# When the samples' steps over the cached values are issued during the prompt's attention

## The chip, the cores and the metric

The kernel runs on one core of one Trainium2 chip. The metric is the time of one whole execution in microseconds (us) as the device measures it; the median of several executions is quoted. The engines are named as the profile names them: PE (TensorE: matrix products), DVE (VectorE), ACT (ScalarE), POOL (GpSimd) and SP (SyncE, which here only starts transfers). Each engine works through its own instructions in their order in the program, and waits at each for what that one needs. Transfers (DMAs) are started from SP and from POOL and run on 16 shared DMA engines; those of one starting engine form that engine's queue.

## What is computed

One inference step of a two-layer decoder trunk, for two groups that share the weights: a prompt of 1024 tokens and 8 samples of one token each. Layer 0 has a mixer that joins an S5 state-space part and a differential attention; layer 1 has another mixer; each layer ends in a feed-forward network (FFN). Only layer 0's attention is touched here. In the reference, cut to what matters:

```python
past = (cache_k[j][page_table]..., cache_v[j][page_table]..., arange(2048))   # samples only
segments = ([] if past is None else [past]) + [(k, v, pos)]
p = softmax(concatenate(scores, axis=-1))
w = p[:, :, 0] - lam * p[:, :, 1]
o = einsum('bhqk,bkhe->bqhe', parts[0], segs[0][1])       # for a sample: the cached values
for wp, (_, v, _) in zip(parts[1:], segs[1:]):
    o = o + einsum('bhqk,bkhe->bqhe', wp, v)              # and its own new value
o = rmsnorm(o, gain) * (1.0 - lam_init)
out = concatenate([s5_out, attn], axis=-1) @ w_out
```

So every sample attends over 2048 cached positions. They lie in pages of 128 positions: 16 pages of keys and 16 pages of values for each sample, scattered over the cache and found through `page_table`. A page of values is 128 x 512 numbers in fp32, 256 KB.

## The kernel before

**Stages of layer 0's mixer** (`mixer0`). First the projections and the S5 scan (the "S5 stage", a loop over 8 blocks `b`). Then the prompt's attention: a loop over 8 heads as the code counts them, position `i` = 0 to 7, which is heads 0 to 3 with the first 512 queries and then heads 0 to 3 with the second 512. Each position has four blocks of 128 queries, so 32 blocks. A block issues the scores of the next block (`attn_scores`, `sc`, L1311 to L1314), transposes its own weights (`pT`, L1341), and the fourth block of a head multiplies them by the values (`po`, L1351). Then comes the last part of the output projection (`out_attn`), and the FFN.

**The samples' steps over the values** (`pv` in `sample_steps`). There are 32: steps 1 to 16 are for samples 0 to 3 and steps 17 to 32 for samples 4 to 7. A step loads four pages of values (`kv<-in_cv`, started on SP at L1383 by `load_page`), one of each of its four samples, and adds four products to one PSUM tile `so` (L1456; the trace has 8 records for a step, an order row "x4" is one step, "x8" two). The pages go through `KV_BUFS` = 8 buffers, so two steps' worth can be under way: the pages of step k+2 can only start when step k has been done. After step 16 and after step 32 the samples' own new values are added (L1462), the sum is copied, transposed (`poT`, L1468) and reduced into `osam`. After step 32 alone `osam` is normalised (`subln`: L769, a chain of small DVE operations, L800, and the result `sd` at L1374), and four POOL transfers (L1481) write it into columns 1024 to 1031 of the four `ao` arrays.

**What reads `ao`.** After the loop `attn_halves(512, 520, range(3))` loads the second 520 columns of `ao[0]` to `ao[2]` on SP (`az`, L1098), which include the samples' columns. SP then loads the eight `x<-xp` (L1075, 516 KB each); `out_attn` loads the samples' columns of `ao[3]` (`azs`, L1111, 4 KB) and needs them for its last quarter (k = 3) of every output. Behind these SP stores eight `xd<-x` (L212) and loads the FFN's first weights (`wst<-in_w_g`, L298).

**Other work between.** `FILL` deals out two further lists of work over the same loop: the S5 part of the output projection (L717 to L719 with `zh`, `zl`, adding to `xr` at L1844) and after it the attention's first half of it (`ahl`, adding to `ax` at L1090). Their loads and stores go through POOL, as do the prompt's `Q` and `K`.

**What sets the order.** Three tables deal out the steps. `KST` and `VST0` say how many steps over keys and values each S5 block issues; `VST[i]` says how many steps over values each of the four blocks of position `i` issues:

```python
v += VST[i]
while v >= 1:
    v -= 1
    vsteps.pop(0)()
```

This is the order in which the code is written. A list scheduler then orders each engine's instructions by its own estimate of when they are ready, so the built program is what counts: before the change, PE has done or has in its order 8, 4, 4, 4, 5, 6, 1 and 0 steps in heads 0 to 7, though the code deals out 4 in the S5 stage, 4 in each of heads 0 to 6 and none in head 7. The steps written in the S5 stage stand behind that stage's last product, at the start of the attention, since they need the softmax of the samples' scores.

Of the kernel before, what the change touches and what calls it, by code (L numbers as in the profile page):

```python
# [62 lines left out]
KV_BUFS = 8  # L63
DENSE = (1, 1, 1, 1, 1, 1, 1, 1)
KST = (3, 3, 2, 2, 2, 2, 2, 0)
VST0 = (0, 0, 0, 0, 0, 0, 0, 4)
FILL = (2, 2, 1.75, 1.75, 1.25, 1.25, 1.25, 1.75)
VST = (1, 1, 1, 1, 1, 1, 1, 0)


def wtile(w):
# [567 lines left out]
class Trunk:  # L639
# [321 lines left out]
    def mixer0(self):  # L961
        tc, nc, a = self.tc, self.nc, self.a
        with ExitStack() as es:
# [17 lines left out]
            with tc.tile_pool(name="smp", bufs=1) as self.kv, ExitStack() as es5:  # L981
# [32 lines left out]
                for b in range(NB):  # L1014
# [8 lines left out]
                    if ksteps == [] and soft:  # L1023
                        soft()
                        soft = None
                    for _ in range(VST0[b]):
                        vsteps.pop(0)()
# [5 lines left out]
                with tc.tile_pool(name="mix", bufs=8) as self.T:  # L1033
# [9 lines left out]
                    for i, (h, G) in enumerate(order):  # L1043
                        nxt = loads[order[i + 1]] if i < 7 else iter(())
                        for qi in range(4):
# [11 lines left out]
                            tail = t  # L1057
                            v += VST[i]
                            while v >= 1:
# [992 lines left out]
```

## Time and profile before

| what | us |
|---|---|
| median of 3 executions | 2332.72 (2327.27 to 2334.79) |
| the profiled execution, its own time | 2325.9 |
| its span in the profile | 2324.1 |
| PE busy in the span | 2194.1 (94%) |
| DVE, ACT, POOL busy | 1605.5, 938.0, 483.3 |
| the prompt's attention with the steps over values | 332 to 640 of the span |

Times of the trace are us from the start of the span. The attention's eight heads lie in it at 333 to 384, 384 to 412, 412 to 440, 440 to 483, 483 to 521, 521 to 568, 568 to 601 and 601 to 636; what follows to about 670 is the output projection's last part. A row of the timeline has start, duration, engine, line, operation, the tiles as out<-in and a count, and in square brackets how long the engine had been idle before it and what it waited for. PE's matrix products overlap, so that the distance between two starts, and not the duration, is the price of one.

### The profile page before, as it was taken

The page shows a single profiled execution, that of the slowest core. Times are in us where ns is not written, and L with a number is a line of the kernel's source. Part 1 is how long each engine was busy: PE and PEld are TensorE (multiplying, and loading weights), DVE is VectorE, ACT ScalarE, POOL GpSimd, SP SyncE. Part 2 cuts the span into 40 slices and gives each one's busy share as a digit, 9 for nine tenths or more (in the row PEclk, how much of TensorE's full clock was granted, in tenths as well). Part 3 has the DMA queues.
Part 4 walks back from the last instruction along what each step waited for, and adds up shares of the span by engine and source line. Part 5 has one row for each costly group of instructions (what it writes and reads, how often), then busy time and mean ns, then how long its engine had stood idle before and what let it go on. Part 6 is the DMA issues. An engine that isn't in the chain of part 4 may idle for free.

```text
span 2324.1 us, 44982 instructions
## 1 busy us (share of the span) xinstructions
PE 2194.1 (94%) x17529; PEld 2061.8 (89%) x17529; DVE 1605.5 (69%) x3090; ACT 938.0 (40%) x1759; POOL 483.3 (21%) x587
## 2 busy tenths in 40 slices
PE   6999988888999999999899999999999999989998
PEld 5978865655688999999899999899899999989997
DVE  8979534544687656566999878664956565689966
ACT  4223234333564333333444365443633333344331
POOL 6132311222203333333000000000233333300001
PEclk8999998989999999999999999999999999999999
DMA  6478978998553212222765321334222122266512
GB/s 222 138 247 271 286 226 233 281 276 227 170 186 119 91 69 84 77 80 91 286 204 189 105 75 50 101 109 143 73 106 83 69 82 83 74 240 216 191 65 74
DMA packets 145798, 348.21 MB, mean 150 GB/s; under 512 B 33513, under 2 KB 40554, under 8 KB 145586
## 3 DMA queue, kind: packets, MB, share of 16 engines
q1 hardware_dynamic: 112226, 246.13, 32.1%
q0 software_dynamic: 32784, 98.69, 13.8%
q8 instruction: 138, 2.26, 0.4%
q14 instruction: 74, 0.61, 0.1%
q10 hardware_dynamic: 576, 0.52, 0.1%
HBM read 281.17 MB, written 64.08 MB: 149 GB/s over the span
## 4 chain that ended last, share of the span: by engine, by line
PE 77%; DVE 11%; DMA 6%; issue 2%; ACT 2%; POOL 1%; SPq 1%; DVEq 0%; ACTq 0%; POOLq 0%
PE pd L719 22%; PE pd L717 22%; PE pd L718 22%; DMA kv<-in_cv 3%; PE pss L1405 1%; DMA kv<-in_ck 1%; PE so L1456 1%; PE po L1351 1%; DVE wp L312 1%; DMA xr<-in_x 1%; PE pT L1341 1%; PE pg L1920 1%; PE pv L1256 1%; PE pv L1257 1%; PE pv L1255 1%
## 5 line engine op out<-in xcount | busy, mean ns | idle before, releaser
L719 PE MATMUL pd<-b,wp 128*128 128x256 f32 (+1 forms) x3496 | 986.5, 283 | 14.5 <-DVE wp L514 13.2
L717 PE MATMUL pd<-b,wp 128*128 128x256 f32 (+1 forms) x3496 | 989.8, 283 | 6.2 <-DVE c L373 2.9
L718 PE MATMUL pd<-b,wp 128*128 128x256 f32 (+1 forms) x3496 | 989.9, 283 | 2.4 <-DVE b L275 2.4
L719 PEld LDWEIGHTS pd<-b,wp 128*128 128x128 f32 x3496 | 661.8, 189 | 15.4 <-DVE wp L514 13.6
L717 PEld LDWEIGHTS pd<-b,wp 128*128 128x128 f32 x3496 | 662.3, 189 | 9.2 <-ACT b L274 2.5
L718 PEld LDWEIGHTS pd<-b,wp 128*128 128x128 f32 x3496 | 662.4, 189 | 3.2 <-DVE b L275 3.2
L331 POOL TENSOR_TENSOR as<-wst 128x512 f32<-128x512 f32 x80 | 135.9, 1699 | 484.0 <-DVE wp L312 328.0
L717 PE MATMUL pd<-xh,wh 128*128 128x344 f32 x576 | 191.3, 332 | 17.4 <-ACT wh L690 8.8
L375 ACT COPY c<-pd 128x512 f32<-128x512 f32 (+1 forms) x260 | 106.1, 444 | 222.6 <-PE pd L719 222.3
L719 PE MATMUL pd<-xh,wl 128*128 128x344 f32 x576 | 188.7, 330 | 4.8 <-DVE wl L691 4.8
L718 PE MATMUL pd<-xl,wh 128*128 128x344 f32 x576 | 190.1, 330 | 0.4 <-DVE xl L829 0.4
L373 DVE TENSOR_TENSOR c<-pd,c 128x512 f32<-128x512 f32 (+1 forms) x214 | 93.2, 470 | 130.6 <-PE pd L719 130.4
L311 ACT CAST wp<-as 128x512 fp32r<-128x512 f32 x176 | 108.9, 622 | 172.6 <-PE pd L719 159.7
L312 DVE TENSOR_TENSOR wp<-wst,wp 128x512 fp32r<-128x512 f32 x122 | 104.1, 855 | 107.4 <-ACT wp L311 107.3
L312 DVE TENSOR_TENSOR wp<-as,wp 128x512 fp32r<-128x512 f32 x176 | 140.5, 801 | 28.2 <-ACT wp L311 28.0
L404 DVE TENSOR_TENSOR c<-c,R 128x1032 f32<-128x1032 f32 x88 | 110.1, 1251 | 44.9 <-ACT c L375 44.9
L717 PEld LDWEIGHTS pd<-xh,wh 128*128 128x128 f32 x576 | 110.8, 192 | 20.5 <-ACT wh L690 8.8
L582 DVE TENSOR_TENSOR x<-pd,x 128x512 f32<-128x512 f32 x160 | 107.8, 684 | 17.9 <-PE pd L719 17.2
L719 PEld LDWEIGHTS pd<-xh,wl 128*128 128x128 f32 x576 | 110.2, 192 | 8.6 <-DVE wl L691 6.0
L718 PEld LDWEIGHTS pd<-xl,wh 128*128 128x128 f32 x576 | 110.6, 192 | 2.7 <-DVE xl L829 0.8
L690 ACT CAST wh<-wst 128x1024 fp32r<-128x1024 f32 x58 | 60.7, 1046 | 105.1 <-PE pd L718 78.9
L691 DVE TENSOR_TENSOR wl<-wst,wh 128x1024 fp32r<-128x1024 f32 x58 | 70.7, 1220 | 44.8 <-ACT wh L690 44.5
(536 smaller groups left out, 4081.5 us busy)
## 6 DMA issues: line engine op xcount, KB each, us to landing
h<-hd SPq DMA_DIRECT2D x82, 516.0 KB, 5.0
kv<-in_ck SPq DMA_DIRECT2D x128, 256.0 KB, 3.9
kv<-in_cv SPq DMA_DIRECT2D x128, 256.0 KB, 6.3
wst<-in_w_d SPq DMA_DIRECT2D x48, 512.0 KB, 4.0
wst<-in_w_g SPq DMA_DIRECT2D x46, 512.0 KB, 3.9
wst<-in_w_up SPq DMA_DIRECT2D x44, 512.0 KB, 3.5
hd<-c POOLq DMA_DIRECT2D x40, 516.0 KB, 3.0
wst<-in_w_o POOLq DMA_DIRECT2D x28, 512.0 KB, 4.1
```

Of the source, the lines that this page charges most:

```text
L311: nc.scalar.copy(W[:, 0], s)
L312: nc.vector.tensor_tensor(W[:, 1], s, W[:, 0].bitcast(F32), ALU.subtract)
L331: (nc.vector if self.first else nc.gpsimd).tensor_tensor(s, x, y, op)
L373: V.tensor_tensor(o, i, o, ALU.add)
L375: A.copy(o, i)
L404: nc.vector.tensor_tensor(x, x, t.R, ALU.mult)
L582: nc.vector.tensor_tensor(y, pt[:, :, :256], y, add)
L690: nc.scalar.copy(H, src)
L691: nc.vector.tensor_tensor(L, src, H.bitcast(F32), ALU.subtract)
L717: mm(p, WH, XH, start=first, stop=False, **kw)
L718: mm(p, WH, XL, start=False, stop=False, **kw)
L719: mm(p, WL, XH, start=False, stop=last, **kw)
```

## The change

Two tables differ. No step is added or taken away, and no load, store or buffer count differs.

```diff
-VST0 = (0, 0, 0, 0, 0, 0, 0, 4)
+VST0 = (0, 0, 0, 0, 0, 0, 0, 0)
 FILL = (2, 2, 1.75, 1.75, 1.25, 1.25, 1.25, 1.75)
-VST = (1, 1, 1, 1, 1, 1, 1, 0)
+VST = (0.5, 1, 1, 1, 1.25, 1.25, 1.25, 0.75)
```

As written, the steps go from 4 in the S5 stage and 4, 4, 4, 4, 4, 4, 4, 0 in the heads to none and 2, 4, 4, 4, 5, 5, 5, 3. In the built program PE now has 6, 2, 2, 4, 4, 6, 5 and 3 of them in heads 0 to 7.

PE at the border from the S5 stage to the attention (`pv` is the last projection of the S5 stage, `sc` the first scores, `so<-kv,ss` two steps over values):

```order
 L1257 MATMUL pv<-wl,xh_196 8x256
-L1456 MATMUL so<-kv,ss 32x512 x8
 L1311 MATMUL sc<-K,Q 128x128
 L1312 MATMUL sc<-K,Q 128x128
@@ -1522,4 +1521,5 @@
 L1314 LDWEIGHTS identb
 L1314 MATMUL sc<-maskb,identb 128x128
+L1456 MATMUL so<-kv,ss 32x512 x8
 L1311 MATMUL sc<-K,Q 128x384
```

Steps 1 and 2 move behind the scores of two blocks. Steps 3 to 6 follow them closely, before as now.

PE in head 6 (position i = 6), before, where step 32 stands alone among one block's scores:

```order
L769 MATMUL psn<-ones,osq 128x1 x4
L1456 MATMUL so<-kv,ss 32x512 x4
L1311 MATMUL sc<-KH,Q 128x512
L1312 MATMUL sc<-KL,Q 128x512
L1311 MATMUL sc<-KH,Q 128x384
L1312 MATMUL sc<-KL,Q 128x384
L1314 LDWEIGHTS identb
L1314 MATMUL sc<-maskb,identb 128x128
L1462 MATMUL so<-vsam,swn 32x512
```

and the same place now, with steps 25 and 26:

```order
L769 MATMUL psn<-ones,osq 128x1 x4
L1456 MATMUL so<-kv,ss 32x512 x4
L1311 MATMUL sc<-KH,Q 128x512
L1312 MATMUL sc<-KL,Q 128x512
L1311 MATMUL sc<-KH,Q 128x384
L1312 MATMUL sc<-KL,Q 128x384
L1314 LDWEIGHTS identb
L1314 MATMUL sc<-maskb,identb 128x128
L1456 MATMUL so<-kv,ss 32x512 x4
L1341 MATMUL pT<-ident,P_8043 128x128
```

Steps 25 and 26 now stand in the head in which step 32 and the samples' closing sum (L1462) stood; steps 27 to 29 follow in the same head and 30 to 32 in head 7.

SP at the end of the attention, before (`ao_112` to `ao_115` are the four `ao`, `xp_116` to `xp_123` the eight `xp`):

```order
L1111 DMA azs<-ao_115 128x8
L298 DMA wst<-in_w_g 128x1024
L1098 DMA az<-ao_112 128x520
L1098 DMA az<-ao_113 128x520
L1098 DMA az<-ao_114 128x520
L1075 DMA x_9243<-xp_116 128x1032
L1075 DMA x_9245<-xp_117 128x1032
```

and now, from the last `x` on:

```order
L1075 DMA x_9255<-xp_122 128x1032
L1075 DMA x_9257<-xp_123 128x1032
L1111 DMA azs<-ao_115 128x8
L212 DMA xd_9259<-x_9243 128x512
L212 DMA xd_9260<-x_9245 128x512
```

The load of the samples' columns of `ao[3]` moves from ahead of the `az` and `x` loads to behind all of them. POOL shows where the writes of the samples' result (L1481) now stand; before, they stood ahead of the store `xp_119<-ax`:

```order
L1087 DMA ax<-xp_122 128x512
L1087 DMA ax<-xp_123 128x512
L1092 DMA xp_122<-ax 128x512
L1481 DMA ao_112<-sd 128x8
L1481 DMA ao_113<-sd 128x8
L1481 DMA ao_114<-sd 128x8
L1481 DMA ao_115<-sd 128x8
L1092 DMA xp_123<-ax 128x512
```

They now come ahead of the very last `xp<-ax`. On PE the samples' L800, which `sd` needs, moves from behind the `po` of head 6 to behind the `po` of head 7. From the third output of `out_attn` on, every engine's order is as before.

## Rows read from the trace of the kernel before

**Rows 1.** The page: the span, and the chain that ended last, by line.

```profile
span 2324.1 us, 44982 instructions
...
PE pd L719 22%; PE pd L717 22%; PE pd L718 22%; DMA kv<-in_cv 3%; PE pss L1405 1%; DMA kv<-in_ck 1%; PE so L1456 1%; PE po L1351 1%; DVE wp L312 1%; DMA xr<-in_x 1%; PE pT L1341 1%; PE pg L1920 1%; PE pv L1256 1%; PE pv L1257 1%; PE pv L1255 1%
```

**Rows 2.** Heads 2, 4, 6, 7: window, length, busy by engine, PE clock, DMA share, GB/s.

```profile
412.00:440.00 28.00, 25.77 (x167) 19.22 (x166) 16.35 (x44) 10.18 (x32) 8.56 (x16) 1.00 1.08 290
...
483.00:521.00 38.00, 30.31 (x181) 21.04 (x180) 20.70 (x42) 14.82 (x37) 6.15 (x12) 0.91 0.92 246
...
568.00:601.00 33.00, 30.93 (x175) 21.78 (x174) 18.97 (x50) 17.06 (x41) 10.06 (x19) 0.95 0.63 160
601.00:636.00 35.00, 32.98 (x187) 23.98 (x186) 22.40 (x55) 18.11 (x45) 6.99 (x13) 1.00 0.44 147
```

**Rows 3.** The value pages' line L1383, 333 to 580: transfers, waits for them, issue to landing.

```profile
L1383 SPq DMA_DIRECT2D kv<-in_cv x120: 332/333/992, 333.1 to 558.9; - x120
...
  PE so L1456: 40.9, 12
...
DMA to landing us min/median/max: 2.6/6.6/13.5
```

**Rows 4.** PE's waits in head 0 and in heads 1 and 2: total, times, longest.

```profile
PE so L1456 <- DMA kv<-in_cv: 16.9, 4, 5.8
...
PE pT L1341 <- DVE xr L1844: 2.1, 1, 2.1
```

**Rows 5.** PE's timeline, steps 18, 20, 26 and 27 (one row x16), 28 and 30.

```profile
458.91 1.94 PE L1456 MATMUL so<-kv,ss 128*32 128x512 f32 x8 [4.70 <-DMA kv<-in_cv]
...
472.20 1.89 PE L1456 MATMUL so<-kv,ss 128*32 128x512 f32 x8 [1.77 <-DMA kv<-in_cv]
...
533.26 1.92 PE L1456 MATMUL so<-kv,ss 128*32 128x512 f32 x16
540.52 1.06 PE L1456 MATMUL so<-kv,ss 128*32 128x512 f32 x8 [0.46 <-DMA kv<-in_cv]
...
553.58 1.93 PE L1456 MATMUL so<-kv,ss 128*32 128x512 f32 x8 [7.76 <-DMA kv<-in_cv]
```

**Rows 6.** PE's timeline in head 6: a step, scores, and two products of the output projection.

```profile
578.98 1.06 PE L1456 MATMUL so<-kv,ss 128*32 128x512 f32 x8
...
580.54 0.34 PE L1311 MATMUL sc<-KH,Q 128*128 128x384 f32 x1
580.71 0.34 PE L1312 MATMUL sc<-KL,Q 128*128 128x384 f32 x1
...
582.43 0.28 PE L719 MATMUL pd<-ahl,wl 128*128 128x256 f32 x1
582.55 0.28 PE L717 MATMUL pd<-ahl,wh 128*128 128x256 f32 x1
```

**Rows 7.** Timelines of DVE, POOL, SP and PE around the border to the output projection.

```profile
607.04 0.25 DVE L1374 SCALAR_TENSOR_TENSOR sd<-osam,subg,psn 128x32 f32<-128x32 f32 x1 [3.59 <-PE psn L800]
...
607.59 1.08 POOL L1481 DMA_DIRECT2D ao<-sd  x2 [13.94 <-DVE sd L1374]
...
628.43 7.98 SPq L1075 DMA_DIRECT2D x<-xp  x7
...
645.86 0.32 SPq L1075 DMA_DIRECT2D x<-xp  x1
...
650.74 1.43 SPq L298 DMA_DIRECT2D wst<-in_w_g  x3
...
631.03 4.90 PE L1351 MATMUL po<-wT,v 128*128 128x512 f32 x14
...
649.51 0.39 PE L717 MATMUL pd<-ahl,wh 128*128 128x260 f32 x1 [0.47 <-DVE x L1126]
```

**Rows 8.** Issue to landing: the eight loads at L1075, then the four writes at L1481.

```profile
DMA to landing us min/median/max: 4.4/8.2/10.9
...
DMA to landing us min/median/max: 1.7/1.7/1.7
```

## The prediction

> **What bounds the kernel now.** I read the page first: the chain that ended last is nearly all products on PE, and 3% of it are the loads of value pages [rows 1]. The change moves only what uses these pages, so the next view is the line that loads them: 120 page loads in the attention, and PE waits 40.9 us for them in 12 waits [rows 3]. That is what an ideal placing could win. The waits by stretch say where they are: 16.9 us, in four, lie in head 0 [rows 4], so 40.9 - 16.9 = 24.0 us in eight waits lie in the later heads. The table by heads then shows the picture that the change answers: heads 2 and 4 run at 290 and 246 GB/s with the DMA share at about 1, heads 6 and 7 at 160 and 147 GB/s with shares of 0.63 and 0.44, and there PE hardly waits [rows 2].
>
> Why PE waits is in the timeline. Eight buffers are two steps' pages, so the loads of step k+2 start when step k is done. I call **need** the time from the end of step k to the moment at which step k+2 can run, and **lead** the work that PE has between the two; a wait is need less lead. Step 18 ends at 458.91 + 1.94 = 460.85 and step 20, which waited, starts at 472.20: need 11.35. Step 28 ends at 541.58 and step 30 waits until 553.58: need 12.0. Step 26 ends at 533.26 + 0.96 and step 28, which hardly waited, starts at 540.52: need 6.3 [rows 5]. A page by itself lands 2.6 us after its issue at the best, 6.6 in the median and 13.5 at the worst [rows 3]: need is mostly what else the DMA engines carry. I take 11, near the two long waits, and keep 6 and 12 as the ends.
>
> **The change, part by part.**
>
> *Steps 1 and 2 behind the scores of two blocks.* The four page waits of head 0 belong to steps 3 to 6, which follow 1 and 2 closely in both programs, so the 16.9 us [rows 4] stay. The loads for steps 3 and 4 start later by what now stands ahead: eight score products and four masks of small blocks, at most 12 times the 0.17 us between two 384-wide ones [rows 6], about 2 us. These scores had to be done anyway and fill PE's time ahead of the first wait, so the shift is paid only where head 0's later part has no other cover. I take +0.5, between 0 and +2.
>
> *Steps 7 to 18, fewer in heads 1 and 2.* Those heads have two steps each instead of four, 8 MB of pages at 0.26 MB each becoming 4 or so. No page wait lies there now; what may go is the waits on other loads, of which `xr` cost 2.1 us in head 2 [rows 4]. Bounds: 0, and twice that, since the chain passes such a load once more in head 3. I take -2.
>
> *Steps 19 to 32, more of them in heads 5 to 7.* Here the lead of each step comes from the order: the products between step k and step k+2, priced by the distance of starts. An example is step 27, in head 6 now: since step 25 PE has four scores of 512 columns (0.23, scaled from 384), four of 384 (0.17), masks and three transposes (together about 0.7), step 26 (1.06) and twelve products of the projection (0.12 each) [rows 6]: 0.92 + 0.68 + 0.7 + 1.06 + 1.44 = 4.8 us. At a need of 11 it waits 6.1. In the same way, with leads of 10.1, 8.9, 9.9, 5.4, 5.4, 4.9 and 7.0, steps 13, 14, 19, 22, 24, 27 and 29 wait 0.9, 2.1, 1.1, 5.6, 5.6, 6.1 and 4.0. Step 32 (lead 6.8) is in the emptiest head, where nothing is loaded behind its pages; with a need of 8 it waits 1.2. The sum is 26.6 us in eight waits. The same rule on the order of before gives 25.5 against the 24.0 measured, so it is fair to about 1.5. The difference is 26.6 - 24.0 = **+2.6**. With need 8 for all, the waits would be 10.5 in sum (-13.5), with 6 they would be 2.3 (-21.7), with 12 about 4 more than before.
>
> Why 11 and not less in the emptier heads: they no longer are empty. Head 6 carries 160 GB/s x 33 us = 5.3 MB now, and five steps' pages are 20 x 0.262 = 5.2 MB more: 10.5 MB in 33 us or 319 GB/s, above the 290 of head 2 [rows 2]. The spread is even over the program's blocks, but two steps still follow each other inside one block, with 5 us of lead.
>
> The Trainium skill, "DMA: Bandwidth & Descriptors", section "Anatomy of one DMA — SWDGE (gpsimd) path", fits one transfer as about 2.0 us plus its bytes at 436 GB/s, for 256 KB an estimate of 2.6 us. That is the least landing of the trace and far under its median [rows 3], so by it alone need would be 6 and the sum the lower end of the first rival.
>
> *The end: the samples' result behind the last `po`.* Before, `sd` was ready at 607.29, 24 us ahead of the last `po`, and the loads of `x` began at 628.43 [rows 7]. Now L800 of the samples stands behind that `po`, which ends at 631.03 + 4.90 = 635.93; `sd` ended 0.4 us behind the `po` ahead of it before, so it comes at 636.4. Its four writes take POOL from 0.3 us later for about 2.2 us [rows 7] and land in 1.7 [rows 8]: 638.4 to 640.6. Each load of `az` waits for one of them, so the first `x` is issued at about 640.6 instead of 628.4, 12 us later. Eight of them at 7.98/7 = 1.14 us take until 649.7, then come `azs` and eight stores at 0.7 us each (before, one load and six stores filled the 4.9 us from 645.86 to 650.74), and the first `wst<-in_w_g` is issued at 650.1 + 5.6 = 655.7, before at 650.74: +5.0 [rows 7]. It is not +12 since SP stood idle before between the seventh `x` and the eighth at 645.86, which waited for `xp`'s last store. PE feels the same amount: `azs`, issued at about 650, needs 1.7 (such a small write) to 8.2 (the median of the `x` loads it now follows) [rows 8]; then ten products and the adds on DVE come before the third output, which began at 649.51 [rows 7]. 650 + 4.4 (the least of the `x` loads) is 654.4, about 5 us behind the 649.51. I take **+5**, with +1 and +12 as ends: below that if the FFN's start has slack, above if `azs` is slow.
>
> **Sum:** +0.5 - 2 + 2.6 + 5 = +6.1 us. On the profiled execution's 2325.9 that is 2332.0. That execution lies at the low end of the three shown, 7 us under the median, so I add the sum to the median: 2332.72 + 6.1 = 2338.8.
>
> **The rivals.**
>
> *Faster: the pages land sooner because they are spread.* If need falls to between 6 and 8 in heads 4 to 7, the waits there shrink by 13.5 to 21.7 us. For it: step 28 needed only 6.3 in head 5 [rows 5], and heads 6 and 7 have idle DMA [rows 2]. Against it: what I said of 319 GB/s, and pairs of steps with 5 us of lead. The end still costs 5. Sum -10 to -18: 2315 to 2323, taken at 2320.
>
> *Slower: `azs` becomes the last thing that PE waits for.* The 4 KB load of `ao[3]`'s sample columns now stands in SP's queue behind 4.1 MB of `x`. If it lands like the `x` loads' median, 8.2 us [rows 8], PE's third output starts at about 650 + 8.2 + 1.5 = 660, 10 us late, and not 5. With needs of 12 in heads 5 and 6, another 2. Sum +11 to +13: 2344 to 2346, and up to 2351 if the FFN's DVE work is pushed too. It decides from the point where `azs` needs over about 5 us. Its split adds to that: on ACT and DVE it now stands behind the FFN's first operands, made from six or seven of the eight `x`, so a late `x` holds it up as well. The same page of the Trainium skill, section "Queues, rings and completion order", says that each DMA engine takes a queue's descriptors in ring order; by that rule a small load can't pass the large ones ahead of it. No row of before shows a small load behind large ones.
>
> *It does little of what it says.* The clustered six steps at the start stay, the pairs stay, and the end may hide in SP's slack (it was idle for 8 us there). Then everything is within 3 us: 2331 to 2335.
>
> **How the numbers follow.** A measurement of this kernel can tell about 0.3%, 7 us, from no change. The forecast, +6.1 with a spread of 5 or so, has 0.50; about two thirds of that are within 7 us (0.34), one third above (0.16). The faster rival has 0.25, nearly all beyond -7 (0.23). The slower one has 0.15. The last has 0.10, of which 0.07 are within and 0.03 below. Faster 0.26, same 0.43, slower 0.31. Range 2317 to 2351: it leaves out the far half of the faster rival and a slower end that costs more than 12.
>
> **What would show it.** PE's waits on `kv` pages outside head 0 should come to 25 to 29 us, the longest in heads 4 to 6; if they are under 15, the faster rival holds. Head 0 keeps 15 to 19. The first `x` is issued 10 to 13 us behind the last `po` minus its old place, and `wst<-in_w_g` 4 to 6 us later against the end of the last `po`. PE then waits for `azs` or its split once, for 3 to 8 us. I am wrong if `sd` is ready well before the last `po`, or if heads 6 and 7 take the pages without waits.

## The result, and the profile after

The changed kernel is slower: 1.0086 times the time of before, 95% interval 1.0066 to 1.0106 (median 2347.45 us against 2328.64 us in the same comparison). A second comparison of the unaltered two kernels gave 1.0103, 1.0087 to 1.0119. So it costs 19 to 24 us. One of the five executions of the changed kernel ran at a granted clock of 0.56 and took 3558 us; the ratio leaves it out. The forecast was 2338.8 us, +6.1, with a range up to 2351: the time lies inside, on the side of the slower rival, and the likeliest case (within 7 us) did not come. That it lies inside is in part luck: the forecast stands on a median of before of 2332.72, 4.1 us above the one that the result is compared with. The top of the range allows +18.3 over that base, and the change costs more than that; in the second comparison its median was 2351.70.

Two profiles of each kernel show where the time went. The table has five moments in us of the span, read from PE's timelines.

| | before | before, again | after | after, again | mean difference of the stretch that ends here |
|---|---|---|---|---|---|
| last product ahead of the attention (`pv`, L1257) | 331.9 | 332.3 | 338.0 | 335.8 | +4.8 |
| row of the last `po` (x14) | 631.0 | 630.5 | 637.3 | 642.3 | +4.2 |
| first product of the FFN | 669.7 | 669.0 | 686.5 | 691.3 | +10.5 |
| end of the span | 2324.1 | 2323.4 | 2342.1 | 2346.8 | +1.2 |

The sum is 20.7. Half of it lies behind the last `po`, in the stretch that answers to [rows 7]. A fifth lies in the attention, and another fifth ahead of it, where PE's order is the same in both; whether that last part costs anything is asked under "What stays open".

The page of the profile after, then PE's waits from 391 to 640, which is all of the attention but its first head (total, times, longest):

```profile
span 2342.1 us, 44981 instructions
```

```profile
PE so L1456 <- DMA kv<-in_cv: 21.2, 7, 7.2
PE pd L717 <- ACT ahl L690: 5.4, 1, 5.4
PE pT L1341 <- DVE xr L1844: 2.1, 3, 1.5
```

In the first head the page waits are

```profile
PE so L1456 <- DMA kv<-in_cv: 18.7, 4, 9.0
```

against 16.9 in [rows 4]. So the whole attention has 39.9 us of page waits after and had 40.9 before [rows 3]: the change moved them and saved next to none. A wait that was not there is the one for `ahl`, the split of the loads `az` of the attention's first half.

The heads that answer to [rows 2], cut at the starts of the `po` of the heads, that is heads 2, 4, 5, 6 and 7 (window, length, busy of PE, PEld, DVE, ACT, POOL, granted clock, DMA share, GB/s):

```profile
417.00:440.00 23.00, 22.64 (x146) 18.00 (x145) 15.33 (x40) 10.03 (x30) 6.12 (x12) 1.00 0.93 290
475.00:506.00 31.00, 29.69 (x182) 20.60 (x181) 21.42 (x47) 15.62 (x38) 8.78 (x17) 1.00 0.99 260
506.00:562.00 56.00, 38.58 (x204) 24.94 (x204) 22.70 (x45) 18.14 (x43) 8.36 (x17) 0.85 0.93 252
562.00:603.00 41.00, 33.80 (x195) 22.08 (x194) 18.37 (x40) 15.65 (x37) 9.81 (x18) 0.92 0.83 235
603.00:636.00 33.00, 31.56 (x202) 21.66 (x201) 20.11 (x54) 16.83 (x40) 4.72 (x9) 1.00 0.45 147
```

Heads 1 to 4 got shorter, 25.9, 23.0, 34.9 and 31.6 us against 27.6, 28.1, 42.7 and 38.5 before: 21.5 us gained (18.9 in the repeated pair). Heads 5 to 7 got longer, 55.9, 40.3 and 33.6 us against 47.1, 32.8 and 29.3: 20.6 us lost (23.2 in the repeated pair). Heads 1 to 4 have five steps fewer and heads 5 to 7 seven more (two come from head 0), at 1.06 us each [rows 6] about 5 and 7 us; most of the rest is waits that changed place.

PE's timeline shows four of them, steps 3, 19, 24 and 27 (the bracket is the idle time and its releaser; a step right behind such a wait takes 1.93 instead of 1.06 us, at a granted clock of 0.50):

```profile
351.95 1.93 PE L1456 MATMUL so<-kv,ss 128*32 128x512 f32 x8 [8.97 <-DMA kv<-in_cv]
...
519.59 1.93 PE L1456 MATMUL so<-kv,ss 128*32 128x512 f32 x8 [7.18 <-DMA kv<-in_cv]
...
552.58 1.94 PE L1456 MATMUL so<-kv,ss 128*32 128x512 f32 x8 [2.44 <-DMA kv<-in_cv]
...
585.49 1.94 PE L1456 MATMUL so<-kv,ss 128*32 128x512 f32 x8 [6.36 <-DMA kv<-in_cv]
```

The end of the attention is what answers to [rows 7]; the timelines of PE, DVE, POOL, SP and ACT there:

```profile
637.28 4.90 PE L1351 MATMUL po<-wT,v 128*128 128x512 f32 x14
...
650.03 0.80 PE L717 MATMUL pd<-ahl,wh 128*128 128x260 f32 x2 [4.02 <-ACT ahl L690]
...
664.16 0.59 PE L717 MATMUL pd<-ahl,wh 128*128 128x260 f32 x1 [5.07 <-ACT ahl L690]
666.51 0.58 PE L717 MATMUL pd<-ahl,wh 128*128 128x260 f32 x1 [0.48 <-DVE x L1126]
...
642.36 0.25 DVE L1374 SCALAR_TENSOR_TENSOR sd<-osam,subg,psn 128x32 f32<-128x32 f32 x1 [5.44 <-PE psn L800]
...
642.90 2.13 POOL L1481 DMA_DIRECT2D ao<-sd  x4 [6.76 <-DVE sd L1374]
...
646.64 1.42 SPq L1098 DMA_DIRECT2D az<-ao  x3
648.22 4.83 SPq L1075 DMA_DIRECT2D x<-xp  x8
654.01 0.32 SPq L1111 DMA_DIRECT2D azs<-ao  x1
...
664.42 1.61 SPq L298 DMA_DIRECT2D wst<-in_w_g  x3
...
659.64 4.38 ACT L260 ACTIVATE b<-x,gains 128x512 fp32r<-128x512 f32 x7
663.93 0.18 ACT L690 CAST ahl<-azs 128x8 fp32r<-128x8 f32 x1
```

The time of `azs` from issue to landing:

```profile
DMA to landing us min/median/max: 9.4/9.4/9.4
```

`sd` is ready 0.4 us behind the last `po` (637.28 + 4.90 = 642.18, and 642.36 + 0.25). Then everything stands in a line: four writes, three `az`, eight `x`, and only then the 4 KB of `azs`, which land 9.4 us behind their issue, at 663.4, 0.2 us behind the last `x`. PE waits twice, 4.0 us for the split of the first `az` and 5.1 us for that of `azs`. The second of these splits stands on ACT behind seven of the FFN's first operands with no idle time between, and `azs` had landed 0.5 us before its turn came (1.4 us in the second profile, 667.4 and 668.8). So the landing and ACT's order come out close together, and ACT's order is the later. From the `po` row to the third output of `out_attn` it takes 666.51 - 637.28 = 29.2 us; before, 649.51 - 631.03 = 18.5 [rows 7].

The waits are only half of it. The stretch from the `po` row to the FFN, before and after (columns as above):

```profile
631.03:669.72 38.69, 34.41 (x251) 30.57 (x249) 27.53 (x47) 22.51 (x42) 0.55 (x1) 1.00 0.86 315
```

```profile
637.28:686.47 49.19, 39.37 (x252) 35.07 (x250) 28.32 (x48) 22.89 (x41) 2.67 (x5) 0.86 0.67 249
```

Of the 10.5 us, 5.5 are idle time of PE (9.8 instead of 4.3) and 5.0 are busy time over the same products. The granted clock is 0.86 instead of 1.00: while PE stood in each of the two waits it fell to 0.50, the lower of its two levels (1.2 instead of 2.4 GHz), and it stayed there from 649.2 to 656.0 and from 662.8 to 669.6. In the second pair of profiles the parts are 7.5 us idle and 3.1 us busy. So a wait here costs its length and, behind it, a stretch at half the clock.

### The profile page after: what moved, and what is told of

It reads as the page before. It is cut to its first block, busy times and chain, and to the rows that moved or that the text cites. A ratio compares the mean times of both kernels' runs of the same rounds, so it can differ in the third digit from the quotient of the medians.

```text
span 2342.1 us, 44981 instructions
## 1 busy us (share of the span) xinstructions
PE 2199.2 (94%) x17529; PEld 2068.1 (88%) x17529; DVE 1605.6 (69%) x3090; ACT 938.9 (40%) x1759; POOL 482.3 (21%) x587
## 4 chain that ended last, share of the span: by engine, by line
PE 77%; DVE 11%; DMA 7%; ACT 2%; issue 2%; POOL 1%; SPq 1%; DVEq 0%; ACTq 0%; POOLq 0%
PE pd L719 22%; PE pd L717 22%; PE pd L718 22%; DMA kv<-in_cv 3%; DMA kv<-in_ck 2%; PE po L1351 1%; PE pss L1405 1%; PE so L1456 1%; DVE wp L312 1%; PE pg L1920 1%; PE pT L1341 1%; PE pv L1256 1%; PE pv L1257 1%; PE pv L1255 1%; DMA xr<-in_x 1%
## 5 line engine op out<-in xcount | busy, mean ns | idle before, releaser
L717 PEld LDWEIGHTS pd<-xh,wh 128*128 128x128 f32 x576 | 111.5, 194 | 20.7 <-ACT wh L690 9.4
L691 DVE TENSOR_TENSOR wl<-wst,wh 128x1024 fp32r<-128x1024 f32 x58 | 70.8, 1221 | 46.9 <-ACT wh L690 46.8
```

Source lines behind the costliest of these rows:

```text
L691: nc.vector.tensor_tensor(L, src, H.bitcast(F32), ALU.subtract)
L717: mm(p, WH, XH, start=first, stop=False, **kw)
```

## The experiments

Every ratio is against the kernel before, run beside it.

**The two kernels once more.** 

> The changed kernel once more, unaltered. Its first profile lay 18.0 us over that of before: the last product ahead of the attention (L1257) started at 338.0 instead of 331.9 (+6.1, in a stretch whose PE order is the same in both), the attention from there to the last po took the same (+0.1), and from the last po to the third output of out_attn it took 10.8 longer. Theory A (the end costs 11 us, the rest is spread of single runs): L1257 falls anywhere between 330 and 338 here, the median is 11 to 15 us over before. Rival B (something ahead of the attention is slower as well): L1257 lies near 338 again, the median is 17 to 20 us over before.

Measured: 1.0103, 1.0087 to 1.0119. The last product ahead of the attention started at 335.8, the last `po` at 642.3, the FFN at 691.3. The end took the same as in the first profile (49.0 us from the `po` row to the FFN, 49.2 there, 38.6 before). The attention itself took 306.5 us, not 299.3. Neither theory holds as it was put: the end is the largest part and is steady, the attention differs by some us between two runs of one program, and the time is above what either said.

> The kernel before once more, for a second profile: how far its own stretches move from run to run. Its first profile had L1257's last product at 331.9 and the last po at 631.0; the five profiles of other kernels, with the same PE order ahead of the attention, had 335.5 to 338.0. Theory A (those few us are spread of single runs, and are given back in the attention's first waits): 332 to 338 here, and the last po within 4 us of 631. Rival B: 330 to 333, so that all the others are truly late there.

Measured: 332.3 and 630.5, as in the first profile. That is what rival B said; theory A reaches it only at its edge.

**The end alone.** The kernel before, with the samples' L800, `sd` and the four writes kept back until behind the last `po`; every step over values stands where it stood:

```diff
+                    def fin():
+                        with self.after(self.lastpo):
+                            self.spread(r, 32, q, d)
+                        nc.vector.scalar_tensor_tensor(dst, o, self.subg, q[:, :32], ALU.mult, ALU.mult)
+                        for h in range(4):
+                            self.qa.dma_start(self.ao[h][:, SEQ:NT], dst[:, h * NS:h * NS + NS])
...
+                    self.fin()
                     for f in (fill, late):
```

> Before, with the tables of before, and only the last part of the samples' result (L800, sd, the four writes) held behind the last po, as in the changed kernel. Theory A: the load azs falls behind the eight x loads, from the last po to the third output 29 us instead of 18.5, in sum +10 to +12 us over before. Rival (the spread of the steps over the heads is what costs): less than +3. Rival B adds nothing here unless the time ahead of the attention moves as well.

Measured: 1.0058, 1.0043 to 1.0073, or 13 us. PE's timeline at the end, then the time of `azs` from issue to landing:

```profile
629.08 4.90 PE L1352 MATMUL po<-wT,v 128*128 128x512 f32 x14
...
658.99 0.59 PE L717 MATMUL pd<-ahl,wh 128*128 128x260 f32 x1 [5.87 <-ACT ahl L690]
661.34 0.58 PE L717 MATMUL pd<-ahl,wh 128*128 128x260 f32 x1 [0.48 <-DVE x L1127]
```

```profile
DMA to landing us min/median/max: 10.2/10.2/10.2
```

The wait for the split of `azs` is there (5.9 us), and the third output begins 32.3 us behind the `po` row. The place of the samples' result alone costs more than half of what the whole change costs. It is not the changed kernel's end in every part: PE also waits 3.6 us at 641.43, for `od` ahead of an L800, which it does not do there.

**The spread without the late end.** The changed kernel, with the last steps dealt out earlier, so that `sd` comes ahead of the last `po` and `azs` ahead of `az` and `x`:

```diff
-VST = (0.5, 1, 1, 1, 1.25, 1.25, 1.25, 0.75)
+VST = (0.5, 1, 1, 1, 1.25, 1.5, 1.75, 0)
```

> The changed kernel with VST (0.5,1,1,1,1.25,1.5,1.75,0): the same steps in heads 0 to 4, and the last ones so early that sd is written ahead of the last po and azs stands ahead of the az and x loads, as before. Theory A: the end is as before (18.5 us from the last po to the third output), and the whole is within 4 us of before. Rival (the spread costs): +8 or more stays. Rival B: +6 stays, with L1257 near 338.

Measured: 1.0083, 1.0061 to 1.0106, or 18 us slower. Theory A falls in this form. The end is as before (38.2 us from the `po` row to the FFN), but the last `po` comes at 645.2, 14 us later than before: heads 5 and 6 now hold 13 steps between them and take 56.0 and 43.1 us. PE's waits in the attention:

```profile
PE so L1456 <- DMA kv<-in_cv: 43.8, 11, 9.9
PE pd L717 <- ACT ahl L690: 6.9, 1, 6.9
PE pT L1341 <- DVE xr L1844: 6.2, 4, 3.7
```

So the spread costs as well, by a longer first wait, by `xr` and by `az`, and the parts don't add up to the whole: 13 and 18 are more than the 19 to 24 of both. A likely reason is that the steps that leave the last head crowd the two ahead of it.

**The start alone.** Before, with no step in the S5 stage, and all steps from 9 on as before:

```diff
-VST0 = (0, 0, 0, 0, 0, 0, 0, 4)
+VST0 = (0, 0, 0, 0, 0, 0, 0, 0)
-VST = (1, 1, 1, 1, 1, 1, 1, 0)
+VST = (2, 1, 1, 1, 1, 1, 1, 0)
```

> Before, with no step in the S5 stage and VST (2,1,1,1,1,1,1,0): steps 1 and 2 stand behind two blocks' scores as in the changed kernel, steps 9 to 32 as before, the end as before. Theory C (the spread costs in heads 5 to 7 and by the late az loads, not at the start): 0 to +4 us against before. Rival (steps 3 to 6 wait longer in head 0: 18.7 to 22.1 us there against 15.2 and 16.8): +4 to +8.

Measured: 1.0016, 1.0003 to 1.0030, or 3.8 us slower. PE's page waits up to the end of the first head:

```profile
PE so L1456 <- DMA kv<-in_cv: 20.0, 4, 9.8
```

That is 3 to 5 us more than in the two profiles of before (16.9 and 14.8), and it agrees with the 3.8. The waits are in the rival's range (18.7 to 22.1), the time is at the top of theory C's. The step that waits longest is step 3. The first of its pages is issued 0.8 us ahead of the first load of `Q` (337.4 and 338.2), in the kernel before 2.1 us ahead (333.1 and 335.2); the loads of `K` and `z` follow those of `Q`. That its pages land later because of them is argued from this and not tried by itself.

**Other queues for az and azs.** The changed kernel with these four loads started on POOL:

```diff
-                    self.qm = getattr(nc, QUEUES[1])
                     X = self.attn_halves(512, 520, range(3))
+                    self.qm = getattr(nc, QUEUES[1])
...
-        self.qm.dma_start(z, self.ao[3][:, SEQ:NT])
+        nc.gpsimd.dma_start(z, self.ao[3][:, SEQ:NT])
```

> The changed kernel with the loads az and azs started on POOL behind the writes of sd, so that SP's x loads wait for neither. Theory A, by its mechanism (x and azs wait in one queue): azs lands 3 to 5 us behind its issue instead of 9.4, the x loads start near 629 to 635 instead of 648, and from the last po to the third output it takes 20 to 24 us instead of 29: 5 to 9 us faster than the changed kernel, 3 to 10 slower than before. If it is the lateness of sd itself that counts, it stays within 3 us of the changed kernel.

Measured: 1.0080, 1.0064 to 1.0095, about 6 us faster than the changed kernel beside it. The mechanism was not the one expected. SP's timeline, then the time of `azs` from issue to landing:

```profile
635.20 19.57 SPq L298 DMA_DIRECT2D wst<-in_w_g  x2
655.00 5.13 SPq L1075 DMA_DIRECT2D x<-xp  x8
```

```profile
DMA to landing us min/median/max: 7.4/7.4/7.4
```

SP's `x` loads don't start early even when nothing of `sd` stands ahead of them: a second load of the FFN's weights stands there, waits 18.8 us for a split on DVE (`wl`, L691) and is issued at 654.4. And `azs`, though its queue now has only the three `az` of 260 KB and one store of 256 KB ahead of it, still lands 7.4 us behind its issue: 0.3 us behind the last `az` of its own queue, and ahead of two of the three `x` that SP had issued before it (663.6 against 663.8 and 665.0).

**A quarter of each page.** In both kernels, 128 of the 512 columns of a page are loaded, and the products read them four times:

```diff
-        d = self.qp.dma_start(dst, src[bass.ds(r, 1)].rearrange("o p n -> (o p) n"))
+        s = src[bass.ds(r, 1)].rearrange("o p n -> (o p) n")
+        if src is self.a["cv"]:
+            dst, s = dst[:, 0:128], s[:, 0:128]
+        d = self.qp.dma_start(dst, s)
...
-                    p[32 * j:32 * j + 32, 0:512], w[:, 32 * j:32 * j + 32], vt[j], start=c == 0, stop=False,
+                    p[32 * j:32 * j + 32, 0:512], w[:, 32 * j:32 * j + 32], vt[j][:, None, 0:128].broadcast_to([128, 4, 128]), start=c == 0, stop=False,
```

> Before, with a quarter of each value page loaded: 128 of its 512 columns, which the products read four times. It leaves out three quarters of the pages' bytes; PE's products keep their sizes, and the scheduler places some steps a little differently. If the page waits come from the bytes on the DMA engines, the waits for pages fall from 41 to under 15 us and the whole is 20 to 35 us faster than before. If they come from the issue of four loads on SP behind one another (1.1 us each), the waits stay over 30 and the gain under 10.

> The changed kernel, with a quarter of each value page loaded, as in the run beside it; the samples' result still comes behind the last po. Theory C (apart from the end's 11 to 13 us, the spread costs by page waits): 9 to 14 us slower than the run beside it, all of it behind the last po. Rival (the spread's cost has another cause, such as the az loads): 18 us slower or more, some 8 of it ahead of the last po.

Measured: 0.9939 (0.9916 to 0.9961) with the tables of before, 0.9990 (0.9980 to 1.0001) with the changed ones. The page line's waits and landings, first before's tables, then the changed ones:

```profile
  PE so L1459: 33.5, 8
...
DMA to landing us min/median/max: 1.7/3.0/12.6
```

```profile
  PE so L1459: 39.8, 11
...
DMA to landing us min/median/max: 1.7/4.4/11.2
```

A page of a quarter lands in about half the time in the median (3.0 against 6.6 us [rows 3] with the tables of before), and PE waits for pages nearly as long. A likely reason is the scheduler: it takes the smaller loads into account and places the steps otherwise, 8, 4, 4, 5, 7, 4, 0 and 0 of them in heads 0 to 7 with the tables of before, and 7, 2, 1, 5, 4, 7, 6 and 0 with the changed ones. So this pair says little on the spread. With the tables of before, 11 to 14 us are gained at 33.5 us of page waits, which fits neither side of the first expectation. The changed tables are 9.5 us slower than those, as theory C said, but not for its reason: in this program the samples' result comes ahead of the last `po`, and the last `po` lies at 625.2 in both. Nor does the pair tell the pages' bytes from the steps' places; the runs with forced places below do that.

**A spread that is even in PE's order.** Since the scheduler gathers the steps, this kernel ties each step on PE behind the last transpose of its block (a head's fifth step behind the block's scores):

```diff
-VST0 = (0, 0, 0, 0, 0, 0, 0, 4)
+VST0 = (0, 0, 0, 0, 0, 0, 0, 0)
-VST = (1, 1, 1, 1, 1, 1, 1, 0)
+VST = (1.25, 1.25, 1.25, 1, 1, 1.25, 1, 0)
...
-                                vsteps.pop(0)()
+                                with self.after(self.lastpt if v < 1 else self.lastsc):
+                                    vsteps.pop(0)()
```

> Before, with no step in the S5 stage, VST (1.25,1.25,1.25,1,1,1.25,1,0), and each step tied on PE behind its block's last transpose (the fifth step of a head behind its block's scores), so that the scheduler can't gather steps: 4, 6, 4, 5, 3, 5, 4 and 1 in heads 0 to 7, nowhere two in a row, the samples' result ahead of the last po and azs ahead of the az and x loads. Theory D (a step waits when PE's work since the step before the last one is less than the 11 us that its pages need, wherever it stands): 9 us of PE's work lie between two steps, 18 between a step and the next but one, so the page waits fall from 41 to under 12 us and the whole is 15 to 30 us faster than before. Rival E (the DMA engines are full in heads 0 and 3 to 5, and a step anywhere there waits): the page waits stay over 25 us and the gain is under 8.

Measured: 0.9996, 0.9983 to 1.0009. PE's waits in the attention:

```profile
PE so L1457 <- DMA kv<-in_cv: 10.8, 3, 5.4
PE pd L717 <- ACT zh L690: 7.9, 1, 7.9
PE pT L1342 <- DVE xr L1845: 5.1, 4, 2.8
PE pd L717 <- ACT ahl L690: 4.7, 2, 3.8
PE sc L1313 <- DMA KL<-kd: 3.9, 2, 2.1
```

This is the run that says most. Theory D is right on the waits and wrong on the time: the page waits fall from 40.9 to 10.8 us as their rule says, and nothing is gained in the whole. Loads that used to be hidden behind the page waits are now what PE waits for: `zh` (the loads `z`), `xr`, `ahl` (the loads `az`), `KL`.

> Before, with nine buffers for pages instead of eight, so that one of the four pages of step k+2 can be loaded ahead of step k's end; the scheduler also moves some steps forward, as the order shows (step 32 ends in head 5). Theory D: each wait shrinks by the one issue that is saved, about 1.1 us of some 3.5: page waits 30 us, 5 to 12 us faster than before. Rival E: within 4 us of before.

Its edit is `KV_BUFS = 9`. Measured: 1.0007, 0.9995 to 1.0018. The page waits fall to 29.0 us, as expected of D, and the time stays: the same lesson with a smaller dose.

**Even spread, a quarter of each page.** Both edits together; the steps stand on PE as in the even spread.

> The kernel with the forced even spread (page waits 10.8 us, but no faster than before), with a quarter of each value page loaded as in the two runs with quarter pages: it leaves out three quarters of the pages' bytes and keeps the place of every step on PE. Theory F (with the page waits gone, PE waits instead for other loads, z, az, KL and xr, which share the DMA engines with the pages; what binds the attention is the traffic as a whole): 8 to 25 us faster than before. Rival G (the other waits are chains that don't depend on the traffic): within 5 us of the even spread with whole pages.

Measured: 0.9907, 0.9882 to 0.9932, or some 20 us less than the even spread with whole pages. The attention from the last `pv` to the row of the last `po`, in the kernel before, in the even spread, and in the even spread with quarter pages (columns as above):

```profile
331.86:631.03 299.17, 249.01 (x1440) 173.89 (x1438) 154.54 (x354) 119.73 (x297) 74.49 (x134) 0.90 0.85 235
```

```profile
336.35:632.78 296.43, 254.87 (x1440) 176.78 (x1437) 153.75 (x354) 119.46 (x297) 74.49 (x134) 0.91 0.88 239
```

```profile
335.35:609.34 273.99, 244.79 (x1439) 172.59 (x1437) 153.41 (x354) 119.57 (x297) 74.50 (x134) 0.94 0.71 171
```

The products are the same in all three. The even spread has 30 us less of page waits, but PE's idle time falls by 8.6 us only (from 50.2 to 41.6) and its busy time grows by 5.9, so the attention is 3 us shorter, less than two profiles of one program differ by; the first two move nearly the same 235 and 239 GB/s. When bytes go, the attention gets 22 us shorter: 12.4 us less idle time, and 10.1 us less busy time at a granted clock of 0.94. With the steps placed as they are in the even spread, theory F is right on the time: the traffic sets a good part of the attention's length. On the single waits it is right in part only. The page waits fall from 10.8 to 4.1 us and those for `KL` go, but `zh`, `xr` and `ahl` keep 15.6 of their 17.7 us.

**Even spread, az earlier.** The four loads `az` of the attention's first half go to SP; on POOL they stand behind the store of head 4's output:

```diff
+        qm, self.qm = self.qm, nc.sync
         X = self.attn_halves(0, 512)
+        self.qm = qm
```

> The kernel with the forced even spread, and the four loads az of the attention's first half, for whose split (ahl) PE waits some 5 us in head 5 in the changed kernel and in the even spread, started on SP instead of behind the store of head 4's output on POOL. If the place in POOL's queue is what makes them late: the wait for ahl in head 5 goes, 2 to 6 us faster than the even spread. If the traffic is: the wait stays within 2 us of 4.7, or comes back at the next load.

Measured: 0.9970, 0.9953 to 0.9987. PE's waits in the attention:

```profile
PE so L1459 <- DMA kv<-in_cv: 9.1, 3, 4.1
PE pd L717 <- ACT zh L690: 6.2, 2, 6.0
...
PE pd L717 <- ACT ahl L690: 1.2, 1, 1.2
```

The wait for `ahl` in the attention falls from 4.7 to 1.2 us. The kernel is 6 us faster than the even spread, as expected of the place in POOL's queue, 7 us faster than before and 27 to 31 us faster than the changed one. It is the only kernel with whole pages here that beats both. (Its profile is of an execution of 2315.6 us; the median is 2322.9.)

## Why the prediction was right or wrong

- **What bounds the kernel: half right.** The 40.9 us of page waits were read rightly, and so was their rule (need less lead): the even spread took 30 of them away just by lead. But I called them what an ideal placing could win, and that is a step that failed: with 30 of them gone the attention was 3 us shorter and the whole no faster. They are where PE happens to wait in a stretch that is full of traffic. A row that hints at it stood in [rows 2]: a DMA share of 0.92 in head 4, where page waits lie, and of 1.08 in head 2.
- **Steps 1 and 2: mis-sized.** +0.5 was forecast, up to +2; the experiment gave 3.8 us, and the first head's page waits rose from 14.8 and 16.9 to 18.7 and more. I priced the shift of the steps and not that their loads now run closer to those of `K`, `Q` and `z`.
- **Fewer steps in heads 1 and 2: wrong.** -2 was forecast for waits on `xr`. In heads 1 and 2 they did go (0.3 us left), but those heads got shorter, PE came to the later `xr` sooner, and they were late in heads 3 and 4 instead: 2.1 us after, as before [rows 4], and 4.7 in the second profile.
- **Steps 13 to 32: right in the sum, wrong in the places, and incomplete.** Forecast: 26.6 us of page waits outside head 0, the longest in heads 4 to 6. Measured: 21.2 us after against 24.0 before. Step 27 was forecast at 6.1 and waited 6.4; steps 22, 24 and 29 were forecast at 5.6, 5.6 and 4.0 and waited 0.9, 2.4 and none; step 19 was forecast at 1.1 and waited 7.2. Step 19 comes right behind the closing sum of samples 0 to 3, whose two copies take page buffers as well; whether that is the cause was not tried. The term left out is the 5.4 us of `ahl`: PE reached the attention's part of the output projection sooner, while its loads stood behind the same store on POOL as before. I had listed POOL's queue only at the end. One figure beside the sum is wrong: with the leads given there a need of 12 makes 33.6 us, 9.6 more than before and not 4.
- **The end: right chain, half the size.** Forecast +5, measured +10.5, and 13 us where it was done alone. Three things make the miss. I took 4.4 us for the landing of `azs`, the least of the `x` loads [rows 8], and it was 9.4, over their median of 8.2; as it was issued 2.2 us sooner behind the `po` row than I had it, it landed 2.8 us later. I then put the third output at the landing, but it begins 3.1 us behind it: the split, the products and the adds were named and not added. And nothing was put down for the clock, which is 3.1 to 5.0 us of the 10.5. A right price for `azs` alone would not have given the time either, since its split waits its turn on ACT. The slower rival asked what happens if it lands like the `x` loads' median and named its split behind the FFN's first operands (659.64 to 664.02 on ACT is that work); this path is what came, and its price for the end was 10. It also says that no row of before shows a small load behind large ones. The trace of before has four of them, the 4 KB loads `zsd` on POOL behind the 512 KB loads of `z`, with the median time to landing in us last:

```profile
z<-zd POOLq DMA_DIRECT2D x4, 512.0 KB, 11.4
z<-zsd POOLq DMA_DIRECT2D x4, 4.0 KB, 9.9
```

With 9.9 us `azs` would have been priced half a us too high. That SP's stores and `wst<-in_w_g` move by about as much was right in kind: forecast +5.0, and 664.42 - 642.18 = 22.2 us behind the `po`'s end against 650.74 - 635.93 = 14.8 before, +7.4.
- **The faster rival fell.** Page waits outside head 0 came to 21.2 us, not under 15. Heads 6 and 7 did take the pages, with one long wait (6.4). The even spread gives a better reason against this rival than I did: it counts page waits alone, and fewer page waits are not less time here.
- **The chances.** 0.31 for slower came true, and 0.43 for no measurable change did not. The sum was several terms away: the end (5.5 us over its forecast), `ahl` (5.4, left out), steps 1 and 2 (3.3) and `xr` (2) came out higher, and the page waits outside head 0 came out 5.4 lower.

On the Trainium skill's page "DMA: Bandwidth & Descriptors": the section "Queues, rings and completion order" says that descriptors are consumed in ring order, and the landing of `azs` 0.2 us behind the last of the eight `x` agrees, in both profiles of the changed kernel and where the end was done alone. The same section says that a DMA's completion is written only after all earlier writes of that DMA engine, across its queues. No run here shows that part: with `azs` on POOL it landed 0.3 us behind the last `az` of its own queue, which the order in the ring already gives.

**What stays open.** In both profiles of before the attention begins at 332, and in all twelve others, two of the changed kernel and ten of the experiments, between 334.9 and 338.0, though PE's order up to there is the same in all but the one with nine buffers. It is 4.8 us of the table's 20.7, it builds up in small steps over the whole stretch, and nothing tried here explains it: it may be the spread of single runs, or something in how the programs are laid out. Nor is it shown to cost anything: the kernel with the end alone started its attention at 336.3 and had its last `po` row at 629.1, the one with nine buffers at 335.2 and 629.0, both ahead of the 631.0 and 630.5 of before. So the first two stretches of the table are better read as one, +9.0 up to the last `po`. And since two profiles of the changed kernel differ by 7 us in the attention, a few us of each stretch can't be given to one cause. The 5.4 us of `ahl` were not taken away in the changed kernel itself, only in the even spread.

## What to carry to other kernels

A wait named in the profile is worth its length only if nothing else is late right behind it: where the DMA share is near 1 in the same stretch, ask which load comes next, and test it by taking bytes away rather than by moving the wait. Before work is moved to the end of a stage, follow its result to whoever reads it and see what it will queue behind; here 4 KB behind 4 MB cost 13 us alone, and the best placing tried won 7. And when a scheduler reorders, a table that is even on paper is even only if the built order is looked at, or forced.

## What the runs showed of the hardware that was not expected

A small load issued behind large ones in one queue lands with the last of them: 4 KB behind 4.1 MB took 9.4, 9.1 and 10.2 us and landed 0.2 us behind the last large load each time. From another queue at the same moment it took 7.4 us and landed with the last of that queue's own loads of 260 KB, ahead of two large loads that the first queue had issued before it. Writes of that size took 1.7 us where the DMA share was 0.16 [rows 8]. Quarter pages landed in 1.7 us at the least and 3.0 to 4.4 in the median, whole ones in 2.6 and 6.6 [rows 3].

Two waits of PE, 4.0 and 5.1 us long, each came with 6.8 us at a granted clock of 0.50, which began before the wait was over; in that stretch PE was busy 5.0 us longer than before over the same products.
